# Two products of a feed-forward output get a pass each, and a norm is applied by fp32 products with a diagonal

## The chip, the cores and the metric

The kernel runs on one core of a Trainium2 chip. A core has a matrix engine (TensorE, PE in the profile; its weight loads are PEld), a vector engine (VectorE, DVE), a scalar engine (ScalarE, ACT), a general engine (GpSimd, POOL) and a queue engine that issues transfers (SyncE, SP). They run side by side and wait for each other by semaphores. The metric is the device time of one execution in microseconds (us), as the median of several runs.

## The reference

One layer of a generator, on 1024 latent tokens and 256 context tokens of width 1024. A mixing part (Fourier, attention and a delta-rule scan over one common input projection) comes first; the change touches the part behind it:

```
mod = jax.nn.silu(c) @ lp['w_mod'] + lp['b_mod']
sh1, sc1, g1, sh2, sc2, g2 = jnp.split(mod[:, None, :], 6, axis=-1)
...
x = x + g1 * _mix_out(P, o_att, o_dn, lp['w_out'], lp['o_norm'])
x = x + g2 * _mlp(_rms(x, lp['norm2']) * (1 + sc2) + sh2, lp['w_ff1'], lp['w_ff2'])

def _rms(x, g):
    y = x * lax.rsqrt(jnp.mean(x * x, axis=-1, keepdims=True) + EPS)
    return y * g

def _mlp(h, w1, w2):                  # (1024, 1024) @ (1024, 4096), then @ (4096, 1024)
    u = jnp.maximum(h @ w1, 0.0)
    return (u * u) @ w2
```

All data are fp32.

## The kernel before

**Precision.** Most products take fp32 operands that are split into two fp32r parts, a high one (a copy that is rounded to fp32r) and a low one (the rest). `mm3` (lines 235 to 238) then makes three matmuls of one product: high by high, high by low, low by high. `split` (line 1488) makes the two parts, with a copy on ACT (`act`, line 220) or DVE and a subtraction on DVE or POOL (line 1490). `mm` (line 233) is one plain matmul, and `tp` (line 241) is a transpose on TensorE with an identity.

**Order.** The code is written for a scheduler: it orders the instructions of each engine's queue by a simulated timeline, in program order unless an instruction isn't ready; `tc.high_priority(n)` moves what stands in it forward. So two instructions next to each other in the code may stand far apart in a queue. Each queue is then worked off in its order.

**Output projection and the norm (lines 1447 to 1561).** The latent rows stand in eight buffers `ACC[q]` of 128 rows by 1024 columns. The output projection runs in four column blocks `n4`; for each row block `q` its product is multiplied with the gate on DVE (1544) and added to `ACC[q]` on POOL (1545). In the last column block each row block is finished: `rms_ff(q)` (1470) forms the sum of squares on ACT and the rate, one over the root of the mean, on POOL (1474 to 1476), into a column of `rsb[q]`, and the row block is stored to DRAM as `x1d[q]` (1549), to be added at the end. When row block 3 is finished, `h2_first` (1492) begins: `norm_ff(0)` scales rows 0 to 3 in place with their rate (line 1480, on DVE), and `h2_T` (1482) transposes them, four blocks of 128 by 128 into one PSUM bank for each of the eight blocks `k` of columns, from where ACT takes them with the scale and shift of the modulation (1486). Then they are split. `norm_ff(1)` scales rows 4 to 7, into the buffers of rows 0 to 3. `h2_second` (1575) transposes these and forms differences with the first half.

**Feed-forward, first product (1602 to 1686).** Both feed-forward products are done by Strassen's scheme in Winograd's form: seven products of half-size blocks in place of eight. `h2_second` forms the sums of activation blocks that it needs, `w1_prep` those of weight blocks (1523, on POOL) and splits them, `ff1` multiplies into one of six PSUM banks and evicts into a ring of 16 half-row buffers `ur`, made of the eight `ACC` buffers (`slot`, 1572, two halves each). In that ring order two halves of row 7 come first, then the first halves of rows 0 to 3. `h2_second` holds its own values in the slots of rows 4 to 6 (1577). The seven left operands of the second product go to DRAM as `usr[n]`.

**Feed-forward, second product (1689 to 1802).** For each of seven products `n` the sum over 4096 is made in 8 pieces `pc` of 512, each with 24 matmuls of 512 columns (four row blocks, two parts, three matmuls). `PASSES` (1714) says which products go through the pieces together: 2 alone, 1 with 3, 4 with 6, 5 with 7. A pass holds its products in four PSUM banks each over its 8 pieces, and loads for each piece its left operands `usr[n]` (1768) and the blocks of `w_ff2` that it needs (1772), through rings of 5 and 12 buffers of 512 KB. DVE forms the sums of weight blocks (1786), and `split` fills a ring of 4 products. After the last piece `product_done` (1731) evicts each row block. `gated` (1727, on POOL) multiplies with the gate and adds the stored rows. For 5 and 7 this is done ahead with the sums formed so far, during their pass; so product 5 is multiplied with two gates on DVE (1752, 1753, through a ring `tmr` of three buffers) and added and subtracted on POOL (1754, 1756), and product 7 takes two operations on DVE (1759, 1760). Then the rows are stored.

Of the kernel before, what the change touches and what calls it, by code (L numbers as in the profile page):

```python
# [14 lines left out]
ALU = mybir.AluOpType  # L15
AX = mybir.AxisListType

P = 128
# [156 lines left out]
def view(b, off, *shape):  # L175
    v = Buf.__new__(Buf)
    v.arena, v.shape, v.at = b.arena, (P,) + shape, b.at + off
    v.n = int(np.prod(shape))
    return v
# [12 lines left out]
def body(tc, t, out):  # L192
# [3 lines left out]
    with ctx:  # L196
# [14 lines left out]
        V, G, T, Y, SC = nc.vector, nc.gpsimd, nc.tensor, nc.sync, nc.scalar  # L211

        def buf(*shape, top=False, a=None, at=None):
            return Buf(a or Fa, (P,) + shape, top, at)
# [4 lines left out]
        def act(o, i, f=AF.Copy, **k):  # L219
            return SC.activation(o, i, f, **k)  # L220
# [5 lines left out]
        def pe(i):  # L226
            return tc.keep_in_program_order(i) if pinned else i
# [4 lines left out]
        def mm(o, l, r, start, stop):  # L232
            pe(T.matmul(o, l, r, start=start, stop=stop))  # L233
# [6 lines left out]
        def tp(o, i):  # L240
            pe(T.transpose(o, i, C["ident"]))  # L241
# [7 lines left out]
        C = {k: cstb[a >= 256]()[:, a % 256 if a < 256 else a - 256 : b if a < 256 else b - 256] for k, (a, b) in CST.items()}  # L249
# [3 lines left out]
        mrowb = [buf(256) for _ in range(2)]  # L253
# [161 lines left out]
        for k, _ in enumerate(mod_steps(0, slabs, bk[2])):  # L415
            b = trb.next()
# [247 lines left out]
        b = gb.next()  # L664
# [9 lines left out]
        b = gb.next()  # L674
# [8 lines left out]
        b = gb.next()  # L683
# [5 lines left out]
        for d in range(2):  # L689
# [3 lines left out]
            for c in range(0, NCA, 16):  # L693
                n = min(16, NCA - c)
                b = gb.next()[:, 0 : n * CK]
# [488 lines left out]
        catF = catD = g1r = None  # L1184
# [197 lines left out]
        def gate_bc(gt_, q, g, c0, bank=bk[2]):  # L1382
            Y.dma_start(gt_, t["b_mod"][:, c0 : c0 + 256].to_broadcast([P, 256]))
            b = bank[:, 0:256]
            mm(b, C["ones"][32 * g : 32 * g + 1, :], mrowb[q]()[32 * g : 32 * g + 1, :], True, True)
            V.tensor_tensor(gt_, b, gt_, op=ALU.add)
# [16 lines left out]
        for n in range(NPR * 5):  # L1403
            j, k = n // 5, n % 5
# [43 lines left out]
        ACC = [b() for b in accb]  # L1448
# [9 lines left out]
        otb = [buf(256) for _ in range(2)]  # L1458
# [4 lines left out]
        rsb = stat.items  # L1463
# [6 lines left out]
        def rms_ff(q):  # L1470
# [4 lines left out]
            G.tensor_scalar(st[:, 0:1], st[:, 0:1], 1.0 / D, EPS, op0=ALU.mult, op1=ALU.add)  # L1475
            G.tensor_tensor(st[:, 1:2], st[:, 0:1], neghalf[:, 0:1], op=ALU.pow)

        def norm_ff(half):
            for n in range(half * 4, half * 4 + 4):
                V.tensor_scalar(ACC[n - half * 4][:, :], ACC[n][:, :], rsb[n]()[:, 1:2], None, op0=ALU.mult)  # L1480

        def h2_T(k, hf):
            b = tr2.next()
            for q in range(4):
                tp(b[:, q * P : (q + 1) * P], ACC[q][:, k * P : (k + 1) * P])
            act(hf, b, AF.Identity, scale=a2()[:, k : k + 1], bias=s2()[:, k : k + 1])

        def split(i, hi, lo, eng, heng=None):
            (heng or act)(hi, i)
            eng.tensor_tensor(lo, i, f32(hi), op=ALU.subtract)  # L1490

        def h2_first():
            norm_ff(0)
            for k in range(KT):
                hf = shr.next()()
                h2_T(k, hf)
                hb = B11 if k < 4 else B21
                split(hf, hb[0]()[:, k % 4], hb[1]()[:, k % 4], G if k % 2 else V, V.tensor_copy)

# [11 lines left out]
        def load_w1(j):  # L1511
            r = [b() for b in rw[j % 2]]
            for d in range(2):
                Y.dma_start(r[d], t["w_ff1"][0, d * 512 : d * 512 + 512, j * 256 : j * 256 + 256].rearrange("(k p) c -> p k c", p=P))
            w1[j] = {f"{f + 1}{d + 1}": r[d][:, :, f * P : f * P + P] for f in range(2) for d in range(2)}
# [12 lines left out]
        for n4 in range(4):  # L1528
# [9 lines left out]
            for q in range(NT):  # L1538
                b = omr.next()[:, 0:256]
# [17 lines left out]
            b.free()  # L1557
        with tc.high_priority(OFN2):
            norm_ff(1)
        for b in g1r + otb + catF + catD:  # L1560
            b.free()


# [6 lines left out]
            hpc += [x for pr_ in prs for x in pr_]  # L1570
            HB[nm] = [(x(), y()) for x, y in prs]
        slot = [view(b, z * 512, 512) for b in accb for z in range(2)]
        ur = Ring(slot[14:16] + slot[0:8:2] + slot[1:8:2] + slot[8:14])

        def h2_second():
            sub = lambda o, i, x: V.tensor_tensor(o, i, x, op=ALU.subtract)
            t1, tr_ = [x() for x in slot[8:12]], Ring([x() for x in slot[12:14]])

            def joined(nm, k):
                b = tr2.next()  # L1580
                for z in range(2):
                    mm(b, idb(), HB[nm][k][z], z == 0, z == 1)
                return b

            for k in range(4):
                h2_T(k, t1[k])
                sub(t1[k], t1[k], joined("11", k))
                split(t1[k], *HB["t1"][k], V)
            for k in range(4):
                h22 = tr_.next()  # L1590
                h2_T(k + 4, h22)
                sub(t1[k], h22, t1[k])
                split(t1[k], *HB["t2"][k], V)
                split(h22, *HB["22"][k], V)
            for k in range(4):
                x3 = tr_.next()
                sub(x3, t1[k], joined("11", k))
                split(x3, *HB["t3"][k], V)
                sub(t1[k], t1[k], joined("21", k))
                split(t1[k], *HB["t4"][k], V)  # L1600
# [56 lines left out]

        with tc.high_priority(OFN3):
            h2_second()
        ORDER = ("11", "12", "s1", "s2", "s4", "s3", "22")  # L1660
        for j in range(2):
            for nm in ORDER[0:2]:
                ff1(j, nm)
        g2b = [buf(512), buf(512)]
        for g in range(4):
            gate_bc(g2b[g // 2]()[:, g % 2 * 256 : g % 2 * 256 + 256], 1, g, 5120 + g * 256, bk[0])
        for nm in ORDER[2:]:
            for j in range(2):
# [4 lines left out]
        def ff1_next(j):  # L1673
            if j < NFF // 2:
                load_w1(j)
                w1_prep(j, *ORDER[0:2])
                for nm in ORDER[0:2]:
                    ff1(j, nm)
# [3 lines left out]
        for j in range(2, NFF // 2):  # L1682
            w1_prep(j, *ORDER[2:])
            for nm in ORDER[2:]:
                ff1(j, nm)
# [25 lines left out]
        banks = A3 + bk  # L1711
        G2 = [b() for b in g2b]
        lo_h, hi_h = slice(0, 512), slice(512, 1024)
        PASSES = (((2,), ("11",)), ((1, 3), ("11", "22", "12")), ((4, 6), ("21", "11", "12")), ((5, 7), ("22", "21")))
        WSUM = {1: ("11", "22", ALU.add), 3: ("12", "22", ALU.subtract), 4: ("21", "11", ALU.subtract), 6: ("12", "11", ALU.add), 7: ("21", "22", ALU.add)}
        WRAW = {2: "11", 5: "22"}
        X1 = {}
# [44 lines left out]

        for pn, (prods, blocks) in enumerate(PASSES):
            for pc in range(NPC):
# [4 lines left out]
                for w in blocks:  # L1769
                    W[w] = raww.next()()  # L1770
                    j, k = int(w[0]) - 1, int(w[1]) - 1
# [7 lines left out]
                if pn == 3 and pc in (2, 3, 4, 5):  # L1779
                    q = pc - 2  # L1780
                    gated(y11[q], q, 0, lo_h)
                    gated(m3[q], q, 0, hi_h)
                for n in prods:
                    if n in WSUM:
                        x, y, op = WSUM[n]
# [38 lines left out]
```

## Time and profile before

| | before |
|---|---|
| median of 3 runs | 1450.36 us (1446.81 to 1450.94) |
| the profiled execution | 1444.78 us, span 1443.0 us |
| granted TensorE clock, mean | 0.985 |
| TensorE busy | 1384.1 us (96%) |
| DVE, ACT, POOL busy | 987.1, 703.4, 645.7 us |
| moved by DMA | 198.46 MB, mean 138 GB/s |

A line of the timeline gives the start in us, the time taken, the engine, the line of the code, the operation, what it writes and reads, and how many instructions were merged; in brackets stands how long the engine sat idle before it and what ended that. A line of groups gives busy time and the mean of one in ns. A line by stretch gives the busy time of each engine with the number of instructions, then the granted clock, the share of the DMA engines and GB/s. Names: `fbase` and `rbase` are the two large SBUF areas for fp32 and fp32r, `z1`, `z2` two smaller ones with a letter for the part of the kernel, `ba` and `bk` PSUM banks. Matmuls overlap, so that the distance from one start to the next, not the time of one, tells their rate.

### The profile page before, as it was taken

To read this page: it belongs to the slowest core of one execution; us is meant where nothing else is said; L and a number is where in the kernel's file an instruction comes from. 1 tells how busy PE (TensorE), PEld (TensorE's weight loads), DVE (VectorE), ACT (ScalarE), POOL (GpSimd) and SP (SyncE) were. 2 spreads that over 40 slices of the span, in tenths; PEclk is the share of its full clock that TensorE was granted. 3 is DMA by queue.
4 is the path that set the end of the run, shared out by engine and by line. 5 is a ranking of instruction groups with operands and counts; after the bars stand their busy time and mean duration, and the time that the engine had idled before them with its cause. 6 is when DMAs were issued, how large, how long until landed. Compare 5 with 4: busy or idle time off the path is not lost.

```text
span 1443.0 us, 28992 instructions
## 1 busy us (share of the span) xinstructions
PE 1384.1 (96%) x11462; PEld 1116.0 (77%) x11462; DVE 987.1 (68%) x1697; ACT 703.4 (49%) x1239; POOL 645.7 (45%) x749
## 2 busy tenths in 40 slices
PE   5899989999999999989899899999999999999997
PEld 1677988867777777777799677888888888888886
DVE  0774679966778777787533987655556676776884
ACT  1742423235777777777313755555455543433331
POOL 2663667763546464484433634434443000000872
PEclk8999999989999999999999999999999999999999
DMA  9873133260000010142322225444446998766641
GB/s 330 327 253 125 45 99 80 63 154 17 9 25 10 10 40 2 37 138 66 105 91 107 84 81 174 162 148 151 135 137 225 323 387 261 237 233 218 197 154 59
DMA packets 143832, 198.46 MB, mean 138 GB/s; under 512 B 51549, under 2 KB 86991, under 8 KB 143439
## 3 DMA queue, kind: packets, MB, share of 16 engines
q1 hardware_dynamic: 142992, 195.91, 41.5%
q8 instruction: 90, 1.47, 0.4%
q10 hardware_dynamic: 703, 0.69, 0.1%
q14 instruction: 47, 0.39, 0.1%
HBM read 150.62 MB, written 45.94 MB: 136 GB/s over the span
## 4 chain that ended last, share of the span: by engine, by line
PE 48%; DVE 3%; DMA 2%; POOL 2%; issue 1%; ACT 0%; SPq 0%; DVEq 0%; POOLq 0%; ACTq 0%
PE bk L237 8%; PE bk L238 8%; PE bk L236 8%; PE ba L236 7%; PE ba L237 7%; PE ba L238 7%; PE bk L233 1%; DMA fbase<-la 1%; DMA la<-fbase 0%; DVE z1b L1355 0%; DMA fbase<-w_out 0%; POOL rbase L1490 0%; DMA fbase<-x 0%; PE bk L241 0%; DVE rbase L1018 0%
## 5 line engine op out<-in xcount | busy, mean ns | idle before, releaser
L220 ACT ACTIVATE rbase<-fbase 128x512 fp32r<-128x512 f32 (+3 forms) x255 | 171.4, 685 | 86.3 <-PE bk L237 55.7
L220 ACT ACTIVATE fbase<-bk 128x512 f32<-128x512 f32 (+3 forms) x224 | 124.9, 561 | 150.6 <-PE bk L233 94.1
L233 PE MATMUL bk<-rbase 128*128 128x256 f32 (+2 forms) x984 | 172.9, 310 | 4.4 <-ACT fbase L220 2.5
L233 PEld LDWEIGHTS bk<-rbase 128*128 128x128 f32 (+1 forms) x984 | 131.7, 174 | 34.1 <-ACT fbase L220 3.3
L220 ACT ACTIVATE z1c<-fbase 128x512 fp32r<-128x512 f32 (+1 forms) x120 | 76.7, 653 | 139.1 <-DMA fbase<-w_ff 53.3
L233 PE MATMUL ba<-rbase 128*65 128x512 f32 (+4 forms) x576 | 138.2, 342 | 5.6 <-DVE rbase L1018 4.3
L1523 POOL TENSOR_TENSOR fbase<-fbase 128x512 f32<-128x512 f32 x64 | 87.4, 1366 | 114.7 <-DVE z1c L1490 89.8
L220 ACT ACTIVATE fbase<-fbase 128x512 f32<-128x512 f32 (+4 forms) x148 | 96.0, 659 | 83.7 <-POOL fbase L1646 27.2
L1728 POOL TENSOR_TENSOR z2c<-z2c,fbase 128x512 f32<-128x512 f32 x16 | 31.1, 1967 | 204.5 <-ACT z2c L220 128.6
L994 DVE TENSOR_REDUCE fbase<-ba 128x1 f32<-128x512 f32 (+1 forms) x192 | 106.4, 594 | 21.3 <-PE ba L233 20.1
L220 ACT ACTIVATE rbase<-z1d 128x1024 fp32r<-128x1024 f32 x61 | 63.0, 1054 | 101.4 <-PE bk L237 86.8
L1490 DVE TENSOR_TENSOR z1c<-fbase,z1c 128x512 fp32r<-128x512 f32 x112 | 91.7, 823 | 24.2 <-ACT z1c L220 20.4
L1490 DVE TENSOR_TENSOR rbase<-z1d,rbase 128x1024 fp32r<-128x1024 f32 x61 | 84.9, 1408 | 32.0 <-ACT rbase L220 31.9
L1018 POOL TENSOR_TENSOR rbase<-fbase,rbase 128x512 fp32r<-128x512 f32 x56 | 72.1, 1287 | 67.5 <-ACT rbase L220 60.0
L236 PE MATMUL bk<-rbase 128*128 128x512 f32 x256 | 99.6, 389 | 0.0
L237 PE MATMUL bk<-rbase 128*128 128x512 f32 x256 | 99.6, 389 | 0.0
L238 PE MATMUL bk<-rbase 128*128 128x512 f32 x256 | 99.6, 389 | 0.0
L1018 DVE TENSOR_TENSOR rbase<-fbase,rbase 128x512 fp32r<-128x512 f32 x104 | 80.1, 770 | 24.4 <-ACT rbase L220 24.0
L1490 DVE TENSOR_TENSOR rbase<-fbase,rbase 128x1024 fp32r<-128x1024 f32 (+1 forms) x65 | 81.1, 1266 | 21.9 <-ACT rbase L220 21.6
L233 PEld LDWEIGHTS ba<-rbase 128*65 128x65 f32 (+1 forms) x576 | 76.1, 154 | 23.6 <-DVE rbase L1018 5.4
L237 PE MATMUL ba<-rbase 128*128 128x512 f32 x192 | 74.7, 389 | 0.0
L238 PE MATMUL ba<-rbase 128*128 128x512 f32 x192 | 74.7, 389 | 0.0
(350 smaller groups left out, 3773.1 us busy)
## 6 DMA issues: line engine op xcount, KB each, us to landing
fbase<-w_ff SPq DMA_DIRECT2D x70, 512.0 KB
u<-fbase SPq DMA_DIRECT2D x112, 256.0 KB
z2a<-w_mod SPq DMA_DIRECT2D x36, 512.0 KB
z1d<-w_ff SPq DMA_DIRECT2D x34, 512.0 KB
z1d<-u SPq DMA_DIRECT2D x33, 512.0 KB
fbase<-u SPq DMA_DIRECT2D x23, 512.0 KB
fbase<-w_in SPq DMA_DIRECT2D x16, 512.0 KB
fbase<-x SPq DMA_DIRECT2D x14, 512.0 KB
```

The source lines that it names most:

```text
L220: return SC.activation(o, i, f, **k)
L233: pe(T.matmul(o, l, r, start=start, stop=stop))
L236: pe(T.matmul(o, lh, rh, start=start, stop=False))
L237: pe(T.matmul(o, lh, rl, start=False, stop=False))
L238: pe(T.matmul(o, ll, rh, start=False, stop=stop))
L994: V.tensor_reduce(st4[:, z : z + 1], b, AX.X, ALU.max)
L1018: (G if k2 in GP and not any(a <= n < b for a, b in NGP) else V).tensor_tensor(hl[:, :, 1], p, f32(hl[:, :, 0]), op=ALU.subtract)
L1490: eng.tensor_tensor(lo, i, f32(hi), op=ALU.subtract)
L1523: G.tensor_tensor(w[nm], w[a], w[b], op=op)
L1728: G.tensor_tensor(c, c, G2[cs_.start // 512], op=ALU.mult)
```

## The change

Products 5 and 7 no longer share a pass: 5 has its own, with block 22 alone, and 7 follows with blocks 22 and 21. Lines that speak of pass 3 (the load of the stored rows and the gating of the earlier sums) now belong to product 5's pass.

The norm is no longer a scaling of the rows. `norm_ff` scales the 128 by 128 identity with the rate of a row block, into one of four small buffers; these lie in a gate buffer `g1r[0]` and in `mrowb[0]`. `h2_T` multiplies the block of `ACC`, as the stationary operand, with that diagonal, as the moving one, in fp32: this transposes and scales at once. Rows 4 to 7 thus stay in their own buffers until `h2_second` has read them; its own values move to the slots of rows 0 to 2, and the ring `ur` begins with row 3. The buffers `g1r` are freed later.

```diff
+        dgb = [view(b, z * P, P) for b in (g1r[0], mrowb[0]) for z in range(2)]
+
         def norm_ff(half):
             for n in range(half * 4, half * 4 + 4):
-                V.tensor_scalar(ACC[n - half * 4][:, :], ACC[n][:, :], rsb[n]()[:, 1:2], None, op0=ALU.mult)
-
-        def h2_T(k, hf):
+                V.tensor_scalar(dgb[n % 4](), C["ident"], rsb[n]()[:, 1:2], None, op0=ALU.mult)
+
+        def h2_T(half, k, hf):
             b = tr2.next()
             for q in range(4):
-                tp(b[:, q * P : (q + 1) * P], ACC[q][:, k * P : (k + 1) * P])
+                mm(b[:, q * P : (q + 1) * P], ACC[half * 4 + q][:, k * P : (k + 1) * P], dgb[q](), True, True)
             act(hf, b, AF.Identity, scale=a2()[:, k : k + 1], bias=s2()[:, k : k + 1])
...
-        for b in g1r + otb + catF + catD:
+        for b in otb + catF + catD:
             b.free()
...
-        ur = Ring(slot[14:16] + slot[0:8:2] + slot[1:8:2] + slot[8:14])
+        ur = Ring(slot[6:16] + slot[0:6])
 
         def h2_second():
-            t1, tr_ = [x() for x in slot[8:12]], Ring([x() for x in slot[12:14]])
+            t1, tr_ = [x() for x in slot[0:4]], Ring([x() for x in slot[4:6]])
...
         with tc.high_priority(OFN3):
             h2_second()
+        for b in g1r:
+            b.free()
...
-        PASSES = (((2,), ("11",)), ((1, 3), ("11", "22", "12")), ((4, 6), ("21", "11", "12")), ((5, 7), ("22", "21")))
+        PASSES = (((2,), ("11",)), ((1, 3), ("11", "22", "12")), ((4, 6), ("21", "11", "12")), ((5,), ("22",)), ((7,), ("22", "21")))
```

The calls of `h2_T` in `h2_first` and `h2_second` pass the half, 0 or 1.

More of the change, by code (lines that the diff above doesn't have):

```diff
@@ L1495, in h2_first @@
                 hf = shr.next()()
-                h2_T(k, hf)
+                h2_T(0, k, hf)
                 hb = B11 if k < 4 else B21
@@ L1585, in h2_second @@
             for k in range(4):
-                h2_T(k, t1[k])
+                h2_T(1, k, t1[k])
                 sub(t1[k], t1[k], joined("11", k))
@@ L1590, in h2_second @@
                 h22 = tr_.next()
-                h2_T(k + 4, h22)
+                h2_T(1, k + 4, h22)
                 sub(t1[k], h22, t1[k])
```

## The prediction

> **What bounds the kernel now.** I read the page first, then the stretches of the two places that the diff touches, then the order of work in them.
>
> ```profile
> span 1443.0 us, 28992 instructions
> PE 1384.1 (96%) x11462; PEld 1116.0 (77%) x11462; DVE 987.1 (68%) x1697; ACT 703.4 (49%) x1239; POOL 645.7 (45%) x749
> PE 48%; DVE 3%; DMA 2%; POOL 2%; issue 1%; ACT 0%; SPq 0%; DVEq 0%; POOLq 0%; ACTq 0%
> ```
>
> TensorE is busy nearly throughout and carries most of the chain that ended last. So an edit counts where it adds TensorE work, where it closes a gap of TensorE, or after the last matmul. The profiled execution took 1444.78 us, its span 1443.0, and the median of the three runs is 1450.36 (1446.81 to 1450.94): the sum below is a difference, made in the span and laid on the median. The three runs lie within 0.3% of each other, so about 0.3% (4.35 us) is what can be told from no change.
>
> The norm sits at the seam between the output projection and the feed-forward part. This is the table by stretch (PE, PEld, DVE, ACT, POOL busy us with instruction counts, granted clock, DMA share, GB/s):
>
> ```profile
> 805.00:810.00 5.00, 4.19 (x21) 3.08 (x21) 4.37 (x4) 0.74 (x2) 4.83 (x6) 1.00 0.00 0
> 810.00:815.00 5.00, 2.67 (x11) 1.57 (x11) 3.96 (x4) 3.82 (x7) 4.15 (x4) 1.00 0.01 3
> 815.00:820.00 5.00, 4.20 (x15) 3.45 (x16) 4.96 (x6) 5.00 (x10) 4.71 (x3) 0.66 0.26 72
> 820.00:825.00 5.00, 3.81 (x23) 2.69 (x22) 5.00 (x9) 4.80 (x9) 0.00 (x0) 1.00 0.56 190
> 840.00:850.00 10.00, 9.43 (x39) 6.76 (x38) 8.86 (x16) 4.99 (x9) 3.27 (x2) 1.00 0.18 55
> 860.00:870.00 10.00, 10.00 (x43) 7.63 (x42) 10.00 (x13) 4.96 (x11) 5.76 (x4) 1.00 0.61 210
> ```
>
> And the same view for the transposes alone (line 241):
>
> ```profile
> 780.00:805.00 25.00, 5.22 (x33) 3.92 (x33) 1.00 0.43 164
> 805.00:825.00 20.00, 5.88 (x31) 4.18 (x31) 0.91 0.21 66
> ```
>
> All 64 transposes of the two halves stand here, 33 while TensorE has no gap and 31 in the one place where it has. Busy time hides part of a gap, because a matmul's latency counts as busy. So I count: full work is 43 matmuls of 512 columns in 10 us, 0.233 each. A transpose takes 0.11 (next fence). From 805 to 825 there are 70 instructions, 31 of them transposes: 39 x 0.233 + 31 x 0.11 = 12.5 us of work in 20, so 7.5 us are lost, 1.4 of them to the clock of 0.66 in the third stretch (0.34 x 4.20). 840 to 850 loses another 0.9 (39 x 0.233 = 9.1). That is 8.4 us of slack in all.
>
> **The norm, part by part.** Removed are 8 DVE scalings of whole rows and 64 transposes; added are 8 scalings of a 128x128 identity and 64 fp32 products with it.
>
> ```profile
> 794.11 0.60 PE L241 MATMUL bk<-fbase 128*128 128x128 f32 x4
> L241 PE MATMUL bk<-fbase x204: 270/272/476, 20.0 to 824.4; 128*128 128x128 f32 x60, 128*64 128x128 f32 x42
> 650.61 1.03 PE L233 MATMUL bk<-fbase 128*128 128x256 f32 x4
> L233 PE MATMUL bk<-fbase,z1b 128*128 128x256 f32 x24 | 6.9, 381 | 0.0
> L233 PEld LDWEIGHTS bk<-fbase,z1b 128*128 128x128 f32 x24 | 4.3, 190 | 0.6
> ```
>
> Four transposes take 0.60, the last one 0.27: (0.60 - 0.27) / 3 = 0.11 from one to the next. The fp32 products of the DFT (line 1322) show the new price. At 650.61 the code issues two products, one for each hp, and the trace holds four records: an fp32 product is two passes, each (1.03 - 0.38) / 3 = 0.217 for 256 columns, so 0.108 for 128 and 0.217 a product. The extra is 64 x (0.217 - 0.11) = **6.8 us** of TensorE, half before 805, half after. Bounds: nothing, if at 128 columns a product took one pass, and 64 x (0.38 - 0.11) = 17.3 if each pass had to wait for a weight load of 0.19. I take 6.8, since the transposes too load weights for every 128 columns and still follow each other at 0.11. The Trainium skill speaks against the change here: its page Perfetto Trace Analysis, Transposes, asks to use the transpose and not a standard matmul for a logical transpose. These rows agree, as far as TensorE's own time goes.
>
> ```profile
> L1480 DVE TENSOR_SCALAR fbase<-fbase 128x1024 f32<-128x1024 f32 x8 | 7.7, 977 | 2.9 <-POOL fbase L1545 1.3 <-POOL fbase L1476 0.9 <-DMA x1d<-fbase 0.4
> L1468 DVE CAST rbase<-fbase 128x128 fp32r<-128x128 f32 x1 | 0.2, 227 | 0.0
> 797.80 0.42 DVE L1544 TENSOR_TENSOR fbase<-ba,fbase 128x256 f32<-128x256 f32 x1
> 803.21 1.81 POOL L1523 TENSOR_TENSOR fbase<-fbase 128x512 f32<-128x512 f32 x1
> 805.44 1.62 POOL L1490 TENSOR_TENSOR rbase<-fbase,rbase 128x512 fp32r<-128x512 f32 x1
> 807.02 0.99 POOL L1476 TENSOR_TENSOR fbase<-fbase 128x1 f32<-128x1 f32 x1
> 808.04 1.77 DVE L1480 TENSOR_SCALAR fbase<-fbase 128x1024 f32<-128x1024 f32 x1 [0.44 <-POOL fbase L1476]
> 809.86 0.44 PE L241 MATMUL bk<-fbase 128*128 128x128 f32 x2 [0.81 <-DVE fbase L1480]
> 809.89 0.60 ACT L220 ACTIVATE fbase<-ba 128x512 f32<-128x512 f32 x1 [4.20 <-DVE fbase L1480]
> 821.46 0.68 DVE L1631 TENSOR_TENSOR fbase<-bk,fbase 128x512 f32<-128x512 f32 x1
> ```
>
> The DVE saves 7.7 - 8 x 0.23 = 5.9 us (the cast of a 128x128 tile is the nearest row for the diagonal). This pays only on a path. The first half's does not: TensorE is full until 805, and the wait of the in-place scaling for the store x1d (0.4) is covered the same way. The second half's does: the rate of row 7 ends at 808.0 on POOL, the scaling holds the first transposes until 809.86, and the diagonal would let them go at about 808.3, **1.5 us** sooner. ACT, too, waited 4.20 for that scaling, because its eviction goes into row 7's buffer; the new ring begins with row 3's halves, free by then. The fourth buffer of the new ring is the second half of row 4, read until the last of the eight column products, where it was a first half, read by the first four. So the eviction at 821.46 can move behind 825, with splits queued behind it on DVE; with six banks for the products TensorE runs on, and I count nothing, at most 1 us.
>
> The first half's 3.4 us of extra passes shift TensorE's arrival at the gaps. What it waits for there is not moved by it: row 7's product was evicted at 797.80, and its rate came 10 us later only because POOL had other work queued. So a later arrival just takes **3.4** out of the gaps. With less waiting, the clock should not fall, and I count **1.2** of its 1.4. Together 6.1 of the 8.4 are recovered; what is left I put down to the second half's own longer passes in a stretch where DVE is at 4.96 and 5.00 of 5. Net of the norm: +6.8 - 6.1 = **+0.7**, with ends -1.6 (all slack recovered) and +6.8 (none).
>
> By the page TensorE: Matmul & The Clock Gate, Part 4 of the Trainium skill, transposes do not count as activity for the clock as matmuls do; products would then keep it full and recover all of the 1.4, which makes the net +0.5. Transposes in a gapped stretch stand beside the 0.66, but the gaps alone could explain it.
>
> **Products 5 and 7.** Before, both end in the last piece, and product 5's epilogue runs after it:
>
> ```profile
> 1426.20 0.69 DVE L1752 TENSOR_TENSOR z2c<-bk,fbase 128x512 f32<-128x512 f32 x1 [9.01 <-PE bk L238]
> 1428.28 1.29 POOL L1756 TENSOR_TENSOR z2c<-z2c 128x512 f32<-128x512 f32 x1
> 1429.61 0.69 DVE L1752 TENSOR_TENSOR z2c<-bk,fbase 128x512 f32<-128x512 f32 x1 [0.55 <-POOL z2c L1756]
> 1434.61 0.69 DVE L1759 TENSOR_TENSOR z2c<-ba,fbase 128x512 f32<-128x512 f32 x1 [0.56 <-POOL z2c L1756]
> 1435.30 0.39 PE L238 MATMUL bk<-rbase 128*128 128x512 f32 x1
> 1438.69 1.28 DVE L1760 TENSOR_TENSOR z2c<-z2c 128x512 f32<-128x512 f32 x2
> 1428.36 11.97 SPq L1725 DMA_DIRECT2D out<-z2c  x8
> ```
>
> The last matmul ends at 1435.7, but DVE only at 1439.97: from 1429 on it waits for POOL, since the products with the gate go through three buffers that two POOL operations of 1.29 per row empty. In the change only product 7 is left there: two DVE operations per row, 0.69 + 0.68 = 1.37, against six matmuls of a row (from 1430.09 to 1435.7 are 24 matmuls, 1.40 a row). So the last row alone trails: 1435.7 + 0.05 + 1.37 = 1437.1, and the store behind it takes what it took, 1439.97 to 1443.0. That is **-2.8 us**. The matmuls, their splits and sums stay the same in number; TensorE has no change of rate to expect.
>
> What moves is product 5's epilogue: to the end of its pass, half way through the old one. Product 7's eight pieces of 24 matmuls take 43.5 at 0.226 (1430.09 to 1435.30 are 23 steps), so it comes at 1392.
>
> ```profile
> 1131.00:1175.00 44.00, 44.00 (x196) 36.43 (x195) 30.98 (x29) 22.60 (x26) 0.00 (x0) 1.00 1.01 377
> 1349.00:1392.00 43.00, 43.00 (x191) 35.60 (x190) 42.52 (x24) 15.57 (x17) 43.00 (x21) 1.00 0.60 200
> 1392.00:1436.00 44.00, 43.69 (x193) 35.85 (x191) 22.11 (x21) 10.04 (x10) 16.58 (x12) 1.00 0.14 53
> 1376.00 23.62 POOL L1729 TENSOR_TENSOR z2c<-z2c,fbase 128x512 f32<-128x512 f32 x11
> 1379.27 2.31 DVE L1490 TENSOR_TENSOR rbase<-z1d,rbase 128x1024 fp32r<-128x1024 f32 x1
> 1415.97 1.22 DVE L1490 TENSOR_TENSOR rbase<-z1d,rbase 128x1024 fp32r<-128x1024 f32 x1
> 1430.09 0.39 PE L236 MATMUL ba<-rbase 128*128 128x512 f32 x1
> ```
>
> **Loads.** W22 is fetched a second time: 8 x 512 KB, 4.2 MB. At the 377 GB/s of the first stretch that is 11 us, and the last two stretches use 0.60 and 0.14 of the DMA engines: hidden. SP gets 8 more issues of about 0.4; product 5's stores now stand among pass 7's loads on SP and wait for POOL there, with these loads behind. The rings hold five pieces of that pass ahead, so I count nothing.
>
> **DVE and POOL.** POOL is full from 1349 on and reaches product 5's adds only after its own queue, at about 1399.6; while it is busy a split of 1.22 takes 2.31. Pass 5 needs two splits per 5.4 us (4.6), pass 7 a sum more (6.9), with 8 gate products between. DVE falls behind then, but splits run ahead: the last ends at 1417.2 and its matmuls start at 1430.1, 12.9 us later. I take nothing, with the bad end among the rivals.
>
> **The sum.** -2.8 + 0.7 = -2.1 us: 1444.78 would become 1442.7, and the median 1450.36 becomes **1448.3**.
>
> **The rivals.** *All slack goes.* The full 8.4 us are recovered instead of 6.1: -2.8 + 6.8 - 8.4 = -4.4, so 1446.0, just on the faster side. For it: DVE loses 5.9 us of work before a stretch where it is the late one, ACT's wait of 4.20 goes, and POOL's queue, which sets row 7's rate, has less DVE work beside it. Against: TensorE would have to run without any gap across a seam. By the GPSIMD Engine Reference, Key points, of the Trainium skill, POOL contends with DVE instructions in a mode with two ports or with two inputs; the splits at 2.31 against 1.22 agree for two inputs, and no run here shows it for scalings.
>
> *Product 5's evictions stall DVE.* This one is slower. If the eight gate products stand in one block on DVE, the fourth waits for POOL's first add, not before 1399.6 + 1.3, and the eighth for the fifth POOL operation, 1399.6 + 5 x 1.29 + 0.69 = 1406.7. All splits of pass 7 are queued behind. TensorE has splits for 12.9 us from 1392, until 1404.9; then come ACT's 1.0 and three DVE operations, 3.7, until 1411.4: 6.5 us of stall. -2.1 + 6.5 = +4.4, so 1454.8. It decides from the point where the block holds DVE beyond about 1400. For it: POOL has no gap in the stretch, and the evictions before it were held in just this way at the end. Against: at the previous pass end the splits were interleaved with the evictions, and scheduling in order of readiness would do so again.
>
> *Weight loads bind the passes.* At 0.19 a pass the extra is 17.3: -2.8 + 17.3 - 8.4 = +6.1, so 1456.5. *The tail does not shorten*, because the stores and not DVE end it: +0.7, so 1451.1.
>
> **How the numbers follow.** Forecast 0.50, all slack 0.27, stall 0.13, weight loads 0.05, tail 0.05. Forecast and tail count as same, all slack as faster, stall and weight loads as slower; since the scatter of the runs is as large as the bound, I move 0.03 from the middle to the slower side. That gives faster 0.27, same 0.52, slower 0.21. The range runs from 1444.5 (all slack, with 1.5 for the scatter) to 1455 (the stall); it leaves out the weight loads and tails of the scatter.
>
> **What would show it.** Right: 64 products as 128 records of line 233 about 0.11 apart in place of line 241 between 780 and 825; less loss between 805 and 825, its clock at 1.00; ACT's wait for 1480 gone; no POOL work after 1430 and DVE done 1.5 us behind the last matmul. Wrong: records 0.19 apart, losses as large as before, or a gap of TensorE after the start of pass 7 with DVE waiting for POOL line 1754.

## The result, and the profile after

The changed kernel takes 1461.9 us (median of four runs, 1460.0 to 1462.9) against 1449.65 (four runs, 1446.81 to 1450.94): a ratio of 1.0094 [1.0078, 1.011], so 11 to 16 us slower. That is outside the forecast range, above its upper end of 1455.0. The profiled execution took 1462.51 us.

The page of the changed kernel (first lines, then the chain's shares by engine):

```profile
span 1460.7 us, 29132 instructions
PE 1400.0 (96%) x11526; PEld 1132.1 (78%) x11526; DVE 989.3 (68%) x1697; ACT 704.5 (48%) x1239; POOL 642.4 (44%) x749
PE 38%; POOL 2%; DVE 1%; DMA 1%; issue 1%; ACT 0%; DVEq 0%
```

There are 64 more records on TensorE, as forecast, and the span is 17.7 us longer. Where these arose shows when the starts of the two traces are subtracted matmul by matmul, by their place in TensorE's queue (the order differs only at the seam and in the passes of products 5 and 7). The last matmul starts at 1435.30 in the kernel before and here, in the timeline, at

```profile
1455.92 0.39 PE L238 MATMUL bk<-rbase 128*128 128x512 f32 x1
1457.11 0.69 DVE L1764 TENSOR_TENSOR z2c<-z2c 128x512 f32<-128x512 f32 x1
```

20.6 us later. Of these 4.65 were there ahead of the seam already, at 711 us, where nothing was changed; every kernel here shows -0.2 to +5.7 there, in part from stretches of low granted clock. From 711 to 886 us the seam adds 9.9. From there to the last pass the difference stays the same to 0.1 us. Pass 7 adds 6.1. The tail gives back 2.9: DVE ends at 1457.8, and the span ends 2.9 after that. Without the part ahead of the seam this is 9.9 + 6.1 - 2.9 = 13.1, against 1449.65 x 0.0094 = 13.6 by the ratio of the timed runs (their medians differ by 12.3). All comparisons below are made in this way: shift at the seam, in pass 7, in the tail.

**The seam**, by stretch as before (PE, PEld, DVE, ACT, POOL busy us with counts, granted clock, DMA share, GB/s):

```profile
805.00:825.00 20.00, 15.81 (x81) 12.47 (x79) 15.87 (x17) 9.04 (x18) 17.59 (x17) 1.00 0.28 92
820.00:825.00 5.00, 1.07 (x6) 0.52 (x4) 3.33 (x3) 2.04 (x4) 3.85 (x3) 1.00 0.26 75
825.00:830.00 5.00, 3.49 (x13) 3.07 (x13) 3.36 (x5) 3.38 (x6) 0.00 (x0) 0.55 0.60 187
830.00:840.00 10.00, 10.00 (x61) 9.12 (x60) 6.19 (x10) 7.69 (x13) 0.00 (x0) 0.88 0.03 10
850.00:860.00 10.00, 7.87 (x34) 6.04 (x34) 9.27 (x14) 4.82 (x9) 1.61 (x1) 1.00 0.18 53
```

The gap did not close. It moved from 810 to 820 and is deeper (1.07 of 5 us busy, 2.67 before), the clock falls behind it to 0.55, and a second gap stands at 850. POOL is busy 17.59 of 20 us where DVE has time to spare (15.87). The price of the products themselves, their groups, row 7's rate, and what ends TensorE's gap:

```profile
803.01 1.95 PE L233 MATMUL bk<-fbase 128*128 128x128 f32 x16
L233 PE MATMUL bk<-fbase 128*128 128x128 f32 x128 | 18.5, 295 | 1.0 <-DVE fbase L1482 1.0
806.46 0.28 PE L238 MATMUL ba<-z1c,rbase 128*128 128x256 f32 x1
818.67 1.00 POOL L1476 TENSOR_TENSOR fbase<-fbase 128x1 f32<-128x1 f32 x1
824.64 1.15 ACT L220 ACTIVATE z1c<-fbase 128x512 fp32r<-128x512 f32 x2 [2.92 <-POOL fbase L1525]
825.69 1.43 ACT L220 ACTIVATE fbase<-bk,fbase 128x512 f32<-128x512 f32 x2
826.51 2.08 PE L233 MATMUL bk<-rbase 128*128 128x512 f32 x4 [4.74 <-ACT fbase L220]
```

128 records for 64 products, (1.95 - 0.28) / 15 = 0.11 apart: two passes each, as forecast. But the output projection's last matmul (third line) starts at 806.46 (797.21 before), 4.6 us later than before beyond the 4.65; row 7's rate comes at 818.67 instead of 807.02, 7.0 later by the same count; and ACT's splits of the weights wait for the weight sums on POOL (line 1525, 1523 before). The last two lines close the chain: TensorE stands for 4.74 us until ACT empties a bank, and that eviction stands in ACT's queue behind two splits that waited 2.92 for POOL's sums. Of the eight sums at the seam five stand ahead of row 7's rate on POOL; in the kernel before it was one.

A count of lost time: each matmul of 512 columns is given 0.233 us, one of 256 0.117, a transpose 0.11, a record of the new products 0.111, and the sum is taken from the time between the same two matmuls, at 711 and 886 us in the kernel before. There it was 159.7 of work and 15.5 lost, in the change 166.9 and 18.2. So 7.2 of the 9.9 are second passes, and instead of 6 us fewer, 2.7 more are lost. Counted as in the prediction, from the clock column and TensorE's busy time, the low clock costs 0.45 x 3.49 + 0.12 x 10.00 = 2.8 us here and 1.4 in the kernel before. So about half of the 2.7 is the clock, and the rest is wider gaps.

**Products 5 and 7.** DVE, TensorE and SP's queue at the start of pass 7, then stretches:

```profile
1405.25 1.23 DVE L1790 TENSOR_TENSOR fbase<-fbase,z1d 128x1024 f32<-128x1024 f32 x1 [8.87 <-DMA fbase<-w_ff]
1409.87 0.79 PE L237 MATMUL ba<-rbase 128*128 128x512 f32 x1 [2.92 <-DVE rbase L1492]
1395.32 0.34 SPq L1729 DMA_DIRECT2D out<-z2c  x1
1395.71 0.42 SPq L1726 DMA_DIRECT2D fbase<-x1d  x1
1396.23 0.40 SPq L1772 DMA_DIRECT2D fbase<-u  x1
1397.56 0.34 SPq L1729 DMA_DIRECT2D out<-z2c  x1
1397.95 0.42 SPq L1726 DMA_DIRECT2D fbase<-x1d  x1
1398.47 0.41 SPq L1776 DMA_DIRECT2D fbase<-w_ff  x1
1390.00:1400.00 10.00, 10.00 (x46) 8.27 (x45) 6.38 (x3) 4.02 (x4) 10.00 (x7) 1.00 0.66 200
1400.00:1410.00 10.00, 7.08 (x32) 5.56 (x30) 4.75 (x4) 4.02 (x4) 8.51 (x7) 0.96 0.98 335
1410.00:1420.00 10.00, 10.00 (x32) 7.97 (x33) 10.00 (x9) 1.96 (x2) 3.63 (x3) 0.70 0.75 247
```

DVE sat idle for 8.87 us, not behind POOL but waiting for a weight block of pass 7. On SP each load stands behind a store of product 4 or 6 and a row load, and the stores wait for the gated adds of POOL (line 1733, four waits of 13.4 us in all from 1375 to 1410), which works without a gap until 1405. TensorE stands for 2.92 us and then runs 10 us at a clock of 0.70 (0.30 x 10 = 3.0): 5.9 of the 6.1.

### The profile page after: what moved, and what is told of

Read it like the earlier page. It is cut to its first block, busy times and chain, and to the rows that moved or that the text cites. A ratio compares the mean times of both kernels' runs of the same rounds, so it can differ in the third digit from the quotient of the medians.

```text
span 1460.7 us, 29132 instructions
## 1 busy us (share of the span) xinstructions
PE 1400.0 (96%) x11526; PEld 1132.1 (78%) x11526; DVE 989.3 (68%) x1697; ACT 704.5 (48%) x1239; POOL 642.4 (44%) x749
```

## The experiments

This table holds what the kernels gave: the ratio to the kernel before, and in us against its trace the shift at the seam, in pass 7 and in the tail, and how much later row 7's rate starts (less the shift ahead of the seam). The ratios come from several executions, the other columns from one trace each; the sums of the shifts agree with the ratios within 2 us. The 15.9 of `pool_queue` arise in the pass of product 5 and not in that of product 7, and the +1.1 in the tail of `second_half_only` behind DVE's last operation.

| | ratio [95%] | seam | pass 7 | tail | rate |
|---|---|---|---|---|---|
| the change | 1.0094 [1.0078, 1.011] | +9.9 | +6.1 | -2.9 | +7.0 |
| norm_alone | 1.0081 [1.0061, 1.0101] | +10.5 | 0 | 0 | +6.3 |
| passes_alone | 1.0011 [0.9999, 1.0022] | +0.2 | +3.3 | -2.5 | -0.3 |
| first_half_only | 1.0045 [1.003, 1.006] | +5.6 | 0 | 0 | +7.8 |
| second_half_only | 1.0024 [1.0006, 1.0042] | +4.0 | 0 | +1.1 | +1.1 |
| identity_products | 1.0074 [1.0048, 1.0099] | +11.0 | 0 | 0 | +7.8 |
| new_slots_only | 1.0007 [0.9991, 1.0022] | +0.7 | 0 | 0 | +1.7 |
| first_half_after_row_5 | 1.0081 [1.0058, 1.0104] | +10.5 | 0 | 0 | +6.3 |
| norm_first_half_last | 1.0055 [1.0034, 1.0076] | +8.2 | 0 | 0 | -8.1 |
| before_first_half_last | 1.0016 [1.0005, 1.0026] | +2.4 | 0 | 0 | -7.9 |
| idle_work_ahead | 1.0036 [1.0026, 1.0046] | +4.6 | 0 | 0 | +8.1 |
| idle_work_behind | 1.0014 [1.0004, 1.0024] | +2.9 | 0 | 0 | -0.2 |
| norm_sums_on_dve | 1.0 [0.9989, 1.0012] | +1.2 | 0 | 0 | +2.0 |
| before_sums_on_dve | 0.9986 [0.9975, 0.9996] | -1.9 | 0 | 0 | -3.4 |
| pool_queue | 1.0087 [1.0064, 1.0109] | -0.8 | +15.9 (pass of 5) | -2.3 | |
| ungated_5 | 0.9985 [0.9974, 0.9995] | -0.4 | 0 | -2.4 | |
| loads_first | 0.9985 [0.9974, 0.9997] | -0.3 | 0 | -2.7 | |
| before_both_moves | 0.9965 [0.9951, 0.9978] | -2.0 | 0 | -2.7 | |
| change_both_moves | 0.9984 [0.9971, 0.9997] | +0.6 | 0 | -2.7 | +1.5 |

### The parts of the change, alone

`norm_alone` is the change with the old `PASSES`; `passes_alone` is the kernel before with the new one. In the other two the diagonal serves one half and the other half is scaled and transposed as before, for the second half with the new slots:

```diff
-                V.tensor_scalar(dgb[n % 4](), C["ident"], rsb[n]()[:, 1:2], None, op0=ALU.mult)
+                if half:
+                    V.tensor_scalar(ACC[n - 4][:, :], ACC[n][:, :], rsb[n]()[:, 1:2], None, op0=ALU.mult)
+                else:
+                    V.tensor_scalar(dgb[n](), C["ident"], rsb[n]()[:, 1:2], None, op0=ALU.mult)
```

> The new norm whole, products 5 and 7 in one pass as before. TensorE's instructions of both traces, set side by side one by one, run the same distance apart from 890 to 1404 us and differ by 9.9 us more behind the seam than ahead of it. So this kernel should be 9 to 10 us slower than before (about 1459.5), with the tail as before. If the loss needed both parts, it would be below 3.

> The pass for each product, norm as before. The same side by side view has 6.1 us of stall at the start of pass 7 and 2.9 us less behind the last matmul: +3.2, about 1452.9. If the stall came only from the seam's later start it would not stand here, and the kernel would be 2.9 us faster.

> Rows 0 to 3 by products with the diagonal, rows 4 to 7 scaled and transposed as before; passes as before. Theory 'order': +6 to +9 us, with row 7's rate some 5 to 7 us later than before. Rival 'second half': +3.4 at most, the bare length of 32 extra passes, or nothing if the gaps take it.

> Rows 0 to 3 scaled and transposed as before, rows 4 to 7 by products with the diagonal; passes as before. Theory 'order': the first half's 32 products stand ahead of the output projection's last rows and push row 7's rate back, and that is the loss; then the seam costs here between -2 and +2 us. Rival 'second half': the doubled passes lie in a stretch where each step waits for the one before; then +5 to +8 us stay here.

The norm loses 10.5 us, the passes 1.0 in sum (0.2 + 3.3 - 2.5); the change, with 13.1, has 2.8 more in pass 7, where its clock is low, and 0.6 less at the seam. Neither half carries the norm's loss alone: 5.6 + 4.0 = 9.6. So the theory that only the first half's order costs time fell, and the rival too. Of the 3.3 in pass 7 of `passes_alone` 1.8 arise at its start, as in the change, and 1.5 from 1416 on, where DVE is full with splits and product 5's evictions between them.

### Passes or buffers

`identity_products` is the kernel before with one line changed, so that the rows are scaled as ever and only the transposes become products:

```diff
-                tp(b[:, q * P : (q + 1) * P], ACC[q][:, k * P : (k + 1) * P])
+                mm(b[:, q * P : (q + 1) * P], ACC[q][:, k * P : (k + 1) * P], C["ident"], True, True)
```

`new_slots_only` is `norm_alone` with transposes of rows that are scaled in place.

> The kernel before, whose 64 transposes of the norm become 64 fp32 products with the plain identity; the scaling of whole rows, the order and the buffers stay. Theory 'passes': the seam loses its time to the second pass of each product, wherever the passes stand, and neither the diagonal nor the new ring of slots matters; then this kernel loses what the norm alone lost, 8 to 12 us. Rival 'buffers': the second half's share, 4 us, comes from the new order of the slots; then it loses 4.5 to 7 us.

> Transposes and scaling of whole rows (rows 4 to 7 in place) as before, but the second half reads rows 4 to 7 and the slots and their ring are those of the change. Theory 'passes': within 1.5 us of the kernel before. Rival 'buffers': 2.5 to 4.5 us slower, with the gap before 817 and the wait for the weights' load after 845 in its trace.

The second pass of each product is enough: +11.0 without any diagonal, +0.7 with all the rest. By the Trainium skill, Perfetto Trace Analysis, Transposes, a logical transpose should be made with the transpose and not with a standard matmul; the trace agrees, with 7.2 us of TensorE's own time and 11 as laid.

### Where the products stand, and what a delay costs

`first_half_after_row_5` calls `h2_first` after row 5 instead of row 3; the next two kernels call it behind the loop over the rows, without its raised priority, with the change's norm and with that of before:

```diff
-                        if q == 3:
-                            h2_first()
...
+        h2_first()
         w1_prep(1, "12")
```

> The change's norm with products 5 and 7 as before, but the first half's columns are written down after row 5 of the output projection and not after row 3. Theory 'order': the products no longer stand ahead of the output projection's last rows, its last matmul comes within 1.5 us of the kernel before and row 7's rate within 2 us; the loss falls from the 11 us of the norm alone to 3 to 6. Rival 'passes': the products cost the same wherever they stand, and the loss stays at 9 to 12.

> The change's norm with products 5 and 7 as before, but the first half's columns are written down behind all rows of the output projection and without their raised priority, so that all 32 products stand behind its last matmul. Theory 'order': the loss beyond the 6.8 us of second passes comes from the output projection's end and with it row 7's rate; now that end comes 2 us or more sooner than in the kernel before, the rate no later than there, and the loss falls from 11 us to 3 to 7. Rival 'chain': the products lie on the path wherever they stand, since the feed-forward products then wait for the columns; the loss stays at 9 to 13.

> The kernel before, with the same move of the first half and nothing else. Theory 'order': an earlier end of the output projection makes row 7's rate earlier and the seam no longer, so between 2 us faster and 1 us slower than the kernel before. Rival 'chain': the feed-forward products wait for their columns, 2 to 6 us slower.

The first edit did nothing: the raised priority pulls the products ahead of the last rows all the same. The second did what it should to the order, the output projection ends 2.1 us sooner and row 7's rate comes 8.1 sooner, and still 8.2 are lost, between the two forecasts. Of these 1.7 are a stretch of low clock at 720 us, ahead of the seam (0.34 x 4.87). So the late rate alone isn't the cause, and this version of my theory fell too. The same move with the transposes costs 2.4, in the rival's range, but its clock (0.60, 0.50 and 0.87 in the three stretches from 815 to 830) by the same count takes 2.9 us more than in the kernel before. Then the same amount of work without any tie to the norm, once ahead of the output projection's end and once behind it:

```diff
+                for _ in range(30 if (n4, q) == (3, 7) else 0):
+                    mm(b, cat(0, 0, q), halves[0][0][:, 0, :], True, True)
...
+            for _ in range(15 if (j, nm) == (0, "12") else 0):
+                mm(b, h[:, 0], hb[0][0], True, True)
```

> The kernel before with 30 more products of 256 columns (3.5 us of TensorE) in the last row block of the output projection, whose results are overwritten and for which nothing waits but that row block; norm and passes are as before. Theory 'arrival', the prediction's: TensorE only arrives 3.5 us later at waits that are set elsewhere, so 0 to 1 us slower. Rival 'chain': the waits behind hang on the end of the output projection, so all of it is paid, 3 to 5 us slower.

> The kernel before with 15 more products of 512 columns (3.5 us) in the second product of the feed-forward part, behind the output projection's end and ahead of the gaps from 809 us on; they too are overwritten, and row 7's rate doesn't depend on them. Theory 'arrival': 0 to 1 us slower. Rival 'chain' in its weak form, in which the waits hang on the output projection's end and row 7's rate alone: also 0 to 1 here, but 3 to 5 for the same work ahead of that end. In its strong form, in which the waits hang on whatever TensorE delivers there: 3 to 5 here too.

By the traces 3.5 us cost 4.6 ahead and 2.9 behind; by the timed runs 5.2 (3.8 to 6.7) and 2.0 (0.6 to 3.5). Part of this is the clock, which by the same count takes 1.2 us more than in the kernel before in the first and 1.4 more in the second. Without it the gaps hide 0.1 of the work ahead and 2.0 of the work behind. So what stands ahead of the output projection's end, as half of the second passes do in the change, is paid in full, and row 7's rate comes 8.1 later. Behind that end, where the rate isn't moved, the gaps hide more than half, and the clock takes most of that back. This is nearer to the rival's weak form than to its strong one.

### What the waits hang on

`w1_prep` sums weight blocks on POOL (line 1525 in the change). For the first two steps `j` these are eight operations (the expectation says ten) at the seam; here they are made on DVE, in `norm_alone` and in the kernel before:

```diff
-                G.tensor_tensor(w[nm], w[a], w[b], op=op)
+                (V if j < 2 else G).tensor_tensor(w[nm], w[a], w[b], op=op)
```

> The norm alone, but the sums of weight blocks for the first two steps of the feed-forward part, ten operations that stand on POOL at the seam, are made on DVE. Theory 'POOL': the waits that stay behind the products hang on POOL's queue, where these sums stand between the last columns' splits and row 7's rate; without them the loss at the seam falls from 10.5 us to 6 or less. Rival 'chain': POOL is only one link of many, DVE takes over as the late one, and the loss stays at 9 to 12.

> The kernel before with the same ten sums on DVE: what the move does without the second passes. Theory 'POOL': row 7's rate comes 4 us or more sooner and the seam is 2 to 5 us shorter than in the kernel before. Rival 'chain': DVE, which is full there, gets longer by ten operations of 0.7 us and the seam is within 1.5 us of the kernel before or longer.

With the second passes in place the norm's loss fell from 10.5 to 1.2, and lost time by the count above from 18.8 to 9.5. The costliest group of POOL in the change from 805 to 825, and then, in `norm_sums_on_dve`, the same sums on DVE and the stretches:

```profile
L1525 POOL TENSOR_TENSOR fbase<-fbase 128x512 f32<-128x512 f32 x8 | 11.2, 1403 | 1.7 <-ACT z1c L220 0.8 <-DVE z1c L1492 0.8
```

```profile
L1525 DVE TENSOR_TENSOR fbase<-fbase 128x512 f32<-128x512 f32 x8 | 6.4, 804 | 0.1
```

```profile
810.00:815.00 5.00, 5.00 (x27) 4.19 (x26) 5.00 (x8) 1.88 (x4) 3.76 (x5) 1.00 0.39 137
815.00:820.00 5.00, 5.00 (x25) 4.12 (x24) 4.93 (x10) 3.37 (x6) 0.42 (x1) 1.00 0.24 60
820.00:825.00 5.00, 4.38 (x22) 2.87 (x21) 3.46 (x6) 3.49 (x7) 0.00 (x0) 1.00 0.80 247
825.00:830.00 5.00, 5.00 (x38) 4.53 (x39) 3.96 (x6) 4.76 (x9) 0.00 (x0) 1.00 0.01 5
```

TensorE is at 1.07 of 5 from 820 to 825 in the change and at 4.38 here, the clock stays at 1.00, and POOL is empty from 820 on. So POOL's queue is what filled the seam's waits: 11.2 us of sums that stood on POOL among the last splits, row 7's add and its rate, each of which comes later when TensorE delivers later. POOL also slows DVE where both work (1.22 against 2.31 in the prediction's rows), and the move ends that too; no run separates the two. But in the change DVE is busy 3.33 of 5 us at the gap, and what TensorE waits for there is the chain by ACT shown above.

In the kernel before the same move brings 1.9 only, and 1.4 of these are the clock, which no longer falls (1.00 in every stretch from 805 to 830). The gaps stay; there DVE is the next that is late (5.00, 5.00 and 5.00 of 5 from 810 to 825). So theory 'POOL' holds for the change, and falls just short of its numbers in the kernel before, where the rival's DVE takes over. Between the two kernels with the move the second passes cost 1.2 + 1.9 = 3.1 of their 7.2 us: 4.1 are hidden.

### The start of pass 7

`pool_queue` gives the row loads and the stores that wait for POOL to POOL's own queue (`G.dma_start` for `Y.dma_start`). `ungated_5` adds product 5 ahead of the gate, so that gate and row loads of the first four row blocks can move into pass 7; `loads_first`, shown here, does so later in pass 7 and also fixes SP's order, the stores of products 4 and 6 behind the last load:

```diff
-                c, d = tmr.next()(), tmr.next()()
-                tt(c, b, G2[1], op=ALU.mult)
-                tt(d, b, G2[0], op=ALU.mult)
-                G.tensor_tensor(m3[q], m3[q], c, op=ALU.add)
-                store(q, 0, hi_h, m3[q])
-                G.tensor_tensor(y11[q], y11[q], d, op=ALU.subtract)
+                tt(m3[q], b, m3[q], op=ALU.add)
+                tt(y11[q], y11[q], b, op=ALU.subtract)
...
-                if pn == 3 and pc == 1:
+                if pn == 4 and pc == 4:
                     x1_load(0, 0, lo_h)
                     x1_load(4, 0, hi_h)
```

> The two passes alone, but the row loads and those stores that wait for POOL are issued from POOL's own queue, so that SP holds only weight loads and the stores of product 7. Theory 'SP blocked': the loads of pass 7 are issued early, the stall at its start (3.3 us) is gone, the tail's gain stays, and the kernel is 1.5 to 3 us faster than the kernel before. Rival 'DMA': the stall comes from the bytes that the 16 DMA engines must move there, which stay; within 1 us of the two passes alone, so 0 to 2 us slower than the kernel before.

> The two passes alone, but product 5 is added to the sums ahead of the gate, so that the row loads and the gate of the first four row blocks move from pass 5 into pass 7 and eight adds of POOL go; SP's order is left to the scheduler, and the stores of products 4 and 6 still stand among the loads. Theory 'SP blocked': the stall at the start of pass 7 shrinks only in part, since the stores stay, 0.5 to 3 us, and the tail's 2.5 us stay gained. Rival 'DMA' (the bytes set the stall, not the queue): 3 us as with the two passes alone.

> The same as the kernel with product 5 added ahead of the gate, but on SP the loads of passes 5 and 7 stand in the order of the pieces, the row loads come after those of the fifth piece of pass 7, and the stores of products 4 and 6 behind the last load; nothing that waits for POOL stands ahead of the loads of pass 7 up to its fifth piece. Theory 'SP blocked': the stall at the start of pass 7 is below 0.5 us, the tail's gain of 2.5 stays, and the kernel is 1.5 to 3 us faster than the kernel before. Rival 'DMA': the same bytes, the same stall, within 1 us of the kernel before or slower.

The remedy by POOL's queue failed: pass 7 has no stall there, but the pass of product 5 ahead of it loses 15.9 us, for a reason of its own (last section). In the other two pass 7 has no stall either. `loads_first`, by stretch:

```profile
1380.00:1390.00 10.00, 10.00 (x46) 8.29 (x45) 7.20 (x8) 4.02 (x4) 0.77 (x1) 1.00 1.04 379
1390.00:1400.00 10.00, 10.00 (x46) 8.29 (x45) 8.65 (x10) 4.02 (x4) 10.00 (x7) 1.00 1.05 394
```

It moves 394 GB/s at a DMA share of 1.05, more than the change does at its stall (335, 0.98), and TensorE never waits: the DMA rival falls. The stall at the start was the queue's. In `ungated_5` the stores still stand among the loads, and it is gone as well, more than I expected: with half of the gated adds moved behind, POOL finishes the others by 1373.4, so that the stores wait no longer. Both kernels also change product 5's evictions, so that they don't tell what removed the later 1.5 us of `passes_alone`.

### Both causes mended

> Scaling and transposes as in the kernel before, the ten weight sums on DVE, products 5 and 7 in a pass each with the loads first and product 5 added ahead of the gate. If the two gains lie on TensorE's path and add up, 1.9 us at the seam and 2.7 in the tail: 4 to 5 us faster than the kernel before, the fastest of all. If one takes the other's place, 2 to 3 us faster.

> The whole change with the same two moves. If POOL's queue and SP's queue were all that stood between the change and its forecast, the seam costs 1 us more than before, pass 7 nothing and the tail gives 2.7: 1 to 2.5 us faster than the kernel before, 12 to 15 us faster than the change. If something else of the change costs time, no faster than the kernel before.

With the sums on DVE and the loads first the change is 0.9984 [0.9971, 0.9997] of the kernel before, in place of 1.0094. Its seam costs 0.6 and the tail gives 2.7. At the seam, and at the start of pass 7:

```profile
815.00:820.00 5.00, 5.00 (x25) 4.10 (x24) 4.93 (x10) 3.42 (x7) 0.07 (x1) 1.00 0.24 62
820.00:825.00 5.00, 4.39 (x23) 2.96 (x22) 3.10 (x5) 3.48 (x7) 0.00 (x0) 1.00 0.79 240
1400.00:1410.00 10.00, 10.00 (x46) 8.29 (x45) 10.00 (x10) 3.15 (x4) 10.00 (x7) 1.00 1.05 398
```

So with the two queues relieved the change's loss of 13 us is gone. The fastest kernel is `before_both_moves`, with scaling and transposes as before: 0.9965 [0.9951, 0.9978], its seam 2.6 us shorter than with the diagonal products. Against it the change still costs these 2.6 us: of 7.2 us of second passes 4.6 are hidden, and 2.6 are paid.

## Why the prediction was wrong, point by point

- *Extra passes, 6.8 us:* right. 128 records 0.11 apart, 7.2 by the count of work.
- *6.1 us of the slack recovered:* this step failed; 2.7 more were lost. It had three terms. "So a later arrival just takes 3.4 out of the gaps" failed: 3.5 us of work without any tie to the norm, ahead of the output projection's end as the first half's products are, cost 4.6, and without the clock's share hid 0.1 of itself. The sentence ahead of it, that row 7's rate came late "only because POOL had other work queued", named the cause and took it as fixed; but in the new order that work grew ahead of the rate, from one weight sum to five. "The clock should not fall" failed with it: 0.55 where it had been 0.66, 1.4 us more and not 1.2 less. And the 1.5 for the diagonal counted from a rate that now came 7 us later. With the weight sums off POOL the seam costs +1.2 in place of the forecast +0.7. That nearness is in part luck: 1.4 us of clock come with the move alone, and against the kernel before with the same move the cost is 3.1.
- *The diagonal saves 5.9 us of DVE:* mis-sized. The eight scalings took 5.6 us and not 1.8 (last section), which leaves 2.1.
- *The clock by products or transposes:* products did not keep it full (0.55), and with the sums off POOL it stays at 1.00 with products and with transposes alike. So here the kind of work did not decide it.
- *Slots, at most 1 us:* right, +0.7.
- *The tail, -2.8:* right, -2.9.
- *Loads, "the rings hold five pieces of that pass ahead, so I count nothing":* this step failed; pass 7 cost 3.3 us alone and 6.1 in the change. The text says that stores and loads stand among each other on SP and that the stores wait for POOL, and then gives the wait no price; it names product 5's stores, where those of products 4 and 6 held the loads up. A ring holds pieces ahead only if the queue that fills it isn't held up.
- *The rival of DVE's evictions, 6.5 us:* pass 7 lost 6.1 in the change, which is near by luck, for the mechanism is another. DVE waited for a load and not for POOL, and the evictions stood between splits; in `passes_alone` they are at most the later 1.5 us.

What stays open: how the loss in POOL's queue is shared between the sums and the buffers they take turns in with the columns of the first half. That pass 7's stall brings a low clock in the change and not in `passes_alone` was seen, not explained; TensorE's gap is 2.92 us in the one and 1.55 at its longest in the other, and no run varied it. Each trace is one execution, so that the clock's shares, 1 to 3 us at the seam, may differ in another.

## What to carry to other kernels

Slack hides extra work only as far as what TensorE waits for there does not itself wait for TensorE; before counting it, ask of each queue on that path (here POOL's) what comes later when the work arrives later, and test it with work whose results nobody uses. Where a load shares a queue with a store, the store's wait is the load's wait: count it even where a ring of buffers looks deep enough. When a large gain is missing, unload the fullest small engine at that place first: eight sums moved from POOL to DVE were worth 9 us of the 10 lost here.

## What the runs showed of the hardware

The diagonal is an eighth of a row block, but its scaling took nearly three quarters of the time: in the change, then the splits of DVE and the timeline of POOL at the place where `pool_queue` stalls:

```profile
L1482 DVE TENSOR_SCALAR fbase<-fbase 128x128 f32<-128x128 f32 x8 | 5.6, 713 | 7.3 <-POOL fbase L1476 7.3
```

```profile
1355.82 17.98 DVE L1490 TENSOR_TENSOR rbase<-z1d,rbase 128x1024 fp32r<-128x1024 f32 x2
```

```profile
1358.86 1.28 POOL L1729 TENSOR_TENSOR z2c<-z2c,fbase 128x512 f32<-128x512 f32 x1
1360.09 2.52 POOL L1728 TENSOR_TENSOR z2c<-z2c,fbase 128x512 f32<-128x512 f32 x2
1370.58 0.55 POOL L1722 DMA_DIRECT2D fbase<-x1d  x1
```

0.71 us a scaling, against 0.98 for a whole row block in the kernel before, while POOL works beside it. In `pool_queue` two splits took 17.98 us, 9 each against 1.22 alone and 2.31 beside POOL in the prediction's rows; meanwhile POOL ran its adds back to back at 1.28, not at the 2.27 that most of them take in the kernel before, and each issue on its queue took 0.55. TensorE stood 6.25 us for that split. The Trainium skill, Trainium Architecture — The Big Picture, What this means for kernel authors, says that the port which DVE and GpSimd share is an exclusive lock and no split of bandwidth; these rows agree, in that one engine is slowed nearly to a stop while the other isn't slowed at all. Why DVE alone is slowed here, and both are elsewhere (2.31 and 2.27), no run shows.
